# Attention's value products and exponential sums as one whole-array fp32 matmul for each head and key tile

## The chip, the cores and the metric

The kernel runs on 1 core of one Trainium2 chip. The metric is device time in microseconds (us) for one execution. The core has five engines that run their own instruction lists in order and wait for each other by semaphores: PE (TensorE, matmuls into PSUM), DVE (VectorE), ACT (ScalarE), POOL (GpSimd) and SP, whose queue issues the DMAs. The profile shows PE's weight loads as an engine of their own, PEld.

## The reference

Two layers work on 1024 latent and 256 context tokens of 1024 channels. Each layer has a modulated RMS norm, one input projection, three token mixers side by side (Fourier mixing, attention, a gated linear recurrence called HGRN), an output projection and a SwiGLU feed-forward part. The change touches the attention alone: 8 query heads, 2 key/value heads, 64 channels each. Latent queries read all 1280 keys; in layer 0 the 256 context queries read the 256 context keys.

```python
def attend(q, k, v):
    s = jnp.einsum('bkgqd,bksd->bkgqs', q, k).astype(jnp.float32) * (HEAD_DIM ** -0.5)
    p = jax.nn.softmax(s, axis=-1).astype(v.dtype)
    return jnp.einsum('bkgqs,bksd->bkgqd', p, v)
```

So for each head and query the kernel needs the exponentials p of its scores, their sum over the keys, the sum over the keys of p times V, and the quotient of the last two.

## The kernel before

The kernel is written in a framework that records the operations in program order and lets a scheduler set the order of each engine's list; tiles live in pools, and a tile waits for a buffer of its pool. `five` is a pool of 25 SBUF buffers of 128 x 1280 fp32. In PSUM it uses eight tiles (banks, in what follows) of 128 x 512 fp32, in four tags of two: `mm`, `sc`, `mx`, `pv`.

Layer by layer, `mixers` projects the inputs, `values` makes V (10 key tiles of 128 keys, both kv heads side by side: 128 keys x 128 columns), `keys` makes K1 and K2, and `queries` the queries. Then come the attention units. A unit is one pair of query heads j (0 to 3; kv head g = j // 2) and one chunk of queries ci: 0 is the 256 context queries, 1 and 2 are 512 latent queries each. Layer 0 has 12 units, layer 1 has 8. `unit_attend` runs over the unit's key tiles kt (10, or 2 for ci = 0): for each of the two heads a, two fp32r matmuls (L631, L632) make the scores `sc` with keys on the partitions, and ACT makes p = exp(scores) (L634). One key tile later follow the value products, L640: for head a the stationary operand is 64 columns of V, the moving operand p (fp32), and the result goes to the half `64*a` of one bank `pv`, so that the two heads stand in the two column halves of the array. After every second key tile come four sums, L645: the stationary operand `first` is 32 columns, a one and 31 zeros, so each adds up p of one head and one key tile in a quarter of the array's columns, into rows 0, 32, 64 and 96 of a second bank `sm`.

At a unit's end ACT copies both banks to SBUF (`pvs`, `sms`), and `unit_finish`, called one key tile into the next unit, lets one matmul with the block matrix `blk` add the quarter sums and spread them over 64 rows (L661). ACT then takes the logarithm and exp(-x) (L663, L664), DVE multiplies (L665), and SP writes the result to `dmix`.

Between the key tiles the loop in `mixers` steps two generators: `unit_prepare` for the unit two ahead, whose matmuls `mx` (L597) and DVE maxima (L598) find a bound for the scores, and `other`, the HGRN and Fourier work, at RATE 1.1 or 1.07 steps for each key tile. HGRN has products `lp` that use quarters of the array (64 x 64), products `ho` with 64 columns (L870) and whole-array products (L851, L855, L867). An fp32 matmul is recorded as two matmuls (two passes), an fp32r matmul as one. L131 to L133 are the three products of the helper `mm3`, which all projections use.

Of the kernel before, what the change touches and what calls it, by code (L numbers as in the profile page):

```python
# [10 lines left out]
F32 = mybir.dt.float32  # L11
F32R = mybir.dt.float32r
U8 = mybir.dt.uint8
AF = mybir.ActivationFunctionType
# [4 lines left out]
P = 128  # L19
# [64 lines left out]
ACB = 5  # L84
# [15 lines left out]
class Kern:  # L100
# [44 lines left out]
    def consts(self):  # L145
        nc, C, I = self.nc, self.C, self.I
        self.c = {}
        cv = self.t2("cv")[0:16, 0:P]
        nc.sync.dma_start(out=cv[0:8], in_=I["c"].rearrange("o (k p) -> (o k) p", p=P))
        nc.sync.dma_start(out=cv[8:16], in_=I["c_ctx"].rearrange("(k p) -> k p", p=P))  # L150
        self.c["ident"] = self.cst.tile([P, P], F32, name="c_ident")
        nc.sync.dma_start(out=self.c["ident"], in_=C["ident"])
        self.last_silu = nc.scalar.activation(out=cv, in_=cv, func=AF.Silu).ins
        ptr = self.ps("mx", "ptc")
        nc.tensor.transpose(ptr[:, 0:16], cv, self.c["ident"][0:16, 0:16])
        sc32 = self.cst.tile([P, KD, 32], F32, name="sc32")
        nc.vector.memset(sc32, 0.0)
        nc.vector.tensor_copy(out=sc32[:, :, 0:2], in_=ptr[:, 0:16].rearrange("p (v k) -> p k v", v=2))
        self.sc32 = sc32
        ones = self.cst.tile([P, P], F32, name="ones")  # L160
        nc.vector.memset(ones, 1.0)
        self.c["ones"] = ones
        first = self.cst.tile([P, 32], F32, name="first")
        nc.vector.memset(first, 0.0)
        nc.vector.memset(first[:, 0:1], 1.0)
        self.c["first"] = first
        eps = self.cst.tile([P, 1], F32, name="eps")
        nc.vector.memset(eps, EPS)
        self.eps = eps
# [369 lines left out]
    def values(self, l):  # L539

        nc = self.nc
        W = 384
        wh, wl = self.wv
        self.V = self.five(f"V{l}", shape=(P, 10, P))
        for t in range(10):
            acc = self.ps("mm", f"v{l}_{t}")
            ts = slice(t * P, (t + 1) * P)
            self.mm3(acc[:, :W], [(self.hh[k][:, ts], self.hl[k][:, ts], wh[k], wl[k]) for k in range(KD)])
            nc.scalar.copy(out=self.V[:, t], in_=acc[:, 0:P])
            vi = self.t2("vi")  # L550
            nc.vector.tensor_copy(out=vi[:, 0:256], in_=acc[:, P:W])
            nc.sync.dma_start(out=self.dv[t], in_=vi[:, 0:256])
# [62 lines left out]
    def unit_attend(self, l, j, ci, Q1, Q2):  # L615


        nc = self.nc
        g = j // 2
        n = CHUNKS[ci][1]  # L620
        nk = 2 if ci == 0 else 10
        pv = self.ps("pv", f"pv{j}_{ci}")
        sm = self.ps("pv", f"sm{j}_{ci}")
        ps = []
        for kt in range(nk + 1):
            if kt < nk:
                ks = slice(kt * P, (kt + 1) * P)
                p = []
                for a in range(2):
                    sc = self.ps("sc", "sc")  # L630
                    nc.tensor.matmul(sc[:, :n], self.K1[g][:, ks], Q1[a], start=True, stop=False)  # L631
                    nc.tensor.matmul(sc[:, :n], self.K2[g][0:66, ks], Q2[a][0:66], start=False, stop=True)  # L632
                    pf = self.t2(f"p{a}", tag="pa", bufs=PAB)[:, :n]
                    nc.scalar.activation(out=pf, in_=sc[:, :n], func=AF.Exp, scale=0.125)  # L634
                    p.append(pf)
                ps.append(p)
            if kt:
                i = kt - 1
                for a in range(2):
                    nc.tensor.matmul(pv[64 * a:64 * a + 64, :n], self.V[:, i, 64 * g:64 * g + 64], ps[i][a], start=(i == 0), stop=(i == nk - 1))  # L640
                if i % 2:
                    for a in range(2):
                        for o in range(2):
                            r = 64 * a + 32 * o
                            nc.tensor.matmul(sm[r:r + 32, :n], self.c["first"], ps[i - 1 + o][a], start=(i == 1), stop=(i == nk - 1), tile_position=(0, r))  # L645
            if kt == DELAY and self.pending:
                self.pending()
                self.pending = None
            yield
        if self.pending:  # L650
            self.pending()
        pvs, sms = [self.t2(nm, tag="acc", bufs=ACB)[:, :n] for nm in ("pvs", "sms")]
        nc.scalar.copy(out=pvs, in_=pv[:, :n])
        nc.scalar.copy(out=sms, in_=sm[:, :n])
        self.pending = lambda: self.unit_finish(j, ci, pvs, sms)

    def unit_finish(self, j, ci, pvs, sms):
        nc = self.nc
        n = CHUNKS[ci][1]
        sm = self.ps("mx", "sm")  # L660
        nc.tensor.matmul(sm[:, :n], self.c["blk"], sms)  # L661
        r = self.t2("ar")[:, :n]
        nc.scalar.activation(out=r, in_=sm[:, :n], func=AF.Ln)  # L663
        nc.scalar.activation(out=r, in_=r, func=AF.Exp, scale=-1.0)  # L664
        nc.vector.tensor_tensor(out=r, in0=pvs, in1=r, op=ALU.mult)  # L665
        nc.sync.dma_start(out=self.dmix[2 + j, :, CHUNKS[ci][0]:CHUNKS[ci][0] + n], in_=r)
# [864 lines left out]
```

## Time and profile before

| | |
|---|---|
| median of 3 runs | 3270.12 us (3266.48 to 3270.54) |
| the profiled execution | 3264.48 us, span 3262.7 us |
| PE busy | 3143.9 us (96%) |
| DVE busy | 1983.9 us (61%) |
| ACT busy | 1403.6 us (43%) |
| POOL busy | 109.0 us (3%) |
| attention of layer 0 | 347 to 780 us of the span |
| attention of layer 1 | 2085 to 2452 us of the span |

A busy PE says only that some matmul was in flight: matmuls are pipelined and their ends are modelled, so they overlap in the records. What a matmul costs PE is better read from starts: from its own start to the start of the next one.

### The profile page before, as it was taken

How to read it: one execution, taken by the hardware profiler on the slowest of the kernel's cores; microseconds unless marked ns; L12 is line 12 of the kernel's file. 1: busy time of each engine (PE TensorE's matmuls, PEld its weight loads, DVE VectorE, ACT ScalarE, POOL GpSimd, SP SyncE). 2: the span in 40 equal slices, each digit the busy share in tenths (PEclk: the TensorE clock that was granted, in tenths of full speed). 3: DMA queues.
4: the chain of work that ended last, by engine and by line, in shares of the span. 5: the costliest groups of instructions: out<-in, count | busy, mean ns of one | idle time of the engine just before them, and what ended most of it. 6: DMA issues, size and time to landing. Idle time of an engine off the chain costs nothing.

```text
span 3262.7 us, 44741 instructions
## 1 busy us (share of the span) xinstructions
PE 3143.9 (96%) x16826; PEld 2322.2 (71%) x16826; DVE 1983.9 (61%) x3459; ACT 1403.6 (43%) x2538; POOL 109.0 (3%) x85
## 2 busy tenths in 40 slices
PE   7999999998979999998999999999999799999998
PEld 4977544455858888886887997544557588887887
DVE  5298766653487666665437427677533876667343
ACT  5255455454353232333335435455453533334343
POOL 1000000000120000000001000000001200000000
PEclk9999999999989999998999999999999899999999
DMA  8356101024314333337645433111025122225453
GB/s 278 110 157 212 49 23 71 20 84 162 118 43 126 97 106 117 108 122 248 189 141 163 147 114 99 54 64 32 30 81 187 49 94 88 80 84 167 147 174 94
DMA packets 358657, 369.51 MB, mean 113 GB/s; under 512 B 21896, under 2 KB 268072, under 8 KB 358440
## 3 DMA queue, kind: packets, MB, share of 16 engines
q1 hardware_dynamic: 358440, 366.65, 35.3%
q8 instruction: 132, 2.16, 0.3%
q14 instruction: 85, 0.70, 0.1%
HBM read 282.00 MB, written 84.41 MB: 112 GB/s over the span
## 4 chain that ended last, share of the span: by engine, by line
PE 84%; DVE 7%; DMA 4%; ACT 3%; issue 1%; SPq 0%; POOL 0%; DVEq 0%; ACTq 0%; POOLq 0%
PE fp L131 8%; PE fp L133 8%; PE fp L132 8%; PE pv L640 6%; PE fd L131 5%; PE fd L133 5%; PE fd L132 5%; PE mx L597 3%; PE sm L645 3%; PE sc L631 3%; PE u L131 3%; PE u L132 3%; PE u L133 3%; PE sc L632 2%; PE oacc L132 2%; PE oacc L131 2%
## 5 line engine op out<-in xcount | busy, mean ns | idle before, releaser
L131 PE MATMUL fd<-a,hwd 128*128 128x512 f32 (+1 forms) x880 | 327.3, 372 | 14.7 <-ACT hwd L124 14.7
L133 PE MATMUL fd<-a,lwd 128*128 128x512 f32 (+1 forms) x880 | 327.6, 372 | 7.2 <-DVE lwd L125 7.0
L132 PE MATMUL fd<-a,hwd 128*128 128x512 f32 (+1 forms) x880 | 325.5, 370 | 0.0
L125 DVE TENSOR_TENSOR lwd<-rwd,hwd 128x512 fp32r<-128x512 f32 (+1 forms) x240 | 158.5, 662 | 267.0 <-ACT hwd L124 258.6
L598 DVE TENSOR_REDUCE mp<-mx 128x1 f32<-128x512 f32 (+1 forms) x400 | 224.1, 591 | 134.0 <-PE mx L597 132.6
L124 ACT CAST hwd<-rwd 128x512 fp32r<-128x512 f32 (+1 forms) x240 | 140.2, 584 | 308.1 <-PE fd L132 173.4
L634 ACT ACTIVATE p<-sc 128x512 f32<-128x512 f32 (+1 forms) x336 | 186.1, 586 | 193.4 <-PE sc L632 185.3
L640 PE MATMUL pv<-p,V 128*64 128x512 f32 (+1 forms) x672 | 232.7, 606 | 0.0
L131 PEld LDWEIGHTS fd<-a,hwd 128*128 128x128 f32 x880 | 167.9, 191 | 43.0 <-ACT hwd L124 15.3
L133 PEld LDWEIGHTS fd<-a,lwd 128*128 128x128 f32 x880 | 167.6, 190 | 37.3 <-DVE lwd L125 9.7
L132 PEld LDWEIGHTS fd<-a,hwd 128*128 128x128 f32 x880 | 167.9, 191 | 27.7 <-issue 0.2
L278 DVE SCALAR_TENSOR_TENSOR as<-wa,sc,as 128x512 f32<-128x512 f32 x224 | 161.3, 748 | 35.5 <-DMA wa<-in_w_ada_dram 34.6
L131 PE MATMUL fp<-mh,hw_gate 128*128 128x512 f32 x352 | 141.1, 401 | 7.0 <-ACT hw_gate L124 7.0
L133 PE MATMUL fp<-mh,lw_gate 128*128 128x512 f32 x352 | 140.1, 398 | 6.3 <-DVE lw_gate L125 6.3
L132 PE MATMUL fp<-ml,hw_gate 128*128 128x512 f32 x352 | 139.3, 396 | 0.0
L131 PE MATMUL fp<-mh,hw_up 128*128 128x512 f32 x352 | 137.8, 392 | 0.0
L132 PE MATMUL fp<-ml,hw_up 128*128 128x512 f32 x352 | 137.7, 391 | 0.0
L133 PE MATMUL fp<-mh,lw_up 128*128 128x512 f32 x352 | 137.0, 389 | 0.0
L131 PE MATMUL u<-a0hh,hwin 128*128 128x512 f32 (+1 forms) x360 | 132.8, 371 | 3.8 <-ACT a0hh L331 2.1
L132 PE MATMUL u<-a0hl,hwin 128*128 128x512 f32 (+1 forms) x360 | 129.4, 361 | 4.1 <-POOL a0hl L329 2.5
L131 PE MATMUL oacc<-mh,hwo 128*128 128x512 f32 (+1 forms) x320 | 121.3, 380 | 9.5 <-ACT mh L124 9.5
L133 PE MATMUL u<-a0hh,lwin 128*128 128x512 f32 (+1 forms) x360 | 127.9, 357 | 0.0
(359 smaller groups left out, 7423.2 us busy)
## 6 DMA issues: line engine op xcount, KB each, us to landing
rwd<-in_w_down_dram SPq DMA_DIRECT2D x200, 256.0 KB
wa<-in_w_ada_dram SPq DMA_DIRECT2D x192, 256.0 KB
rw_gate<-in_w_gate_dram SPq DMA_DIRECT2D x44, 512.0 KB
rw_up<-in_w_up_dram SPq DMA_DIRECT2D x44, 512.0 KB
da<-mw_gate SPq DMA_DIRECT2D x88, 256.0 KB
ar<-da SPq DMA_DIRECT2D x88, 256.0 KB
rwin<-in_w_in_dram SPq DMA_DIRECT2D x30, 512.0 KB
rwo<-in_w_out_dram SPq DMA_DIRECT2D x24, 512.0 KB
```

The lines of the kernel that those rows point to most:

```text
L124: self.nc.scalar.copy(out=hi, in_=src)
L125: self.nc.vector.tensor_tensor(out=lo, in0=src, in1=hi, op=ALU.subtract)
L131: self.nc.tensor.matmul(out, lh, rh, start=(first and i == 0), stop=False)
L132: self.nc.tensor.matmul(out, lh, rl, start=False, stop=False)
L133: self.nc.tensor.matmul(out, ll, rh, start=False, stop=(last and i == n - 1))
L278: nc.vector.scalar_tensor_tensor(out=acc, in0=w, scalar=sc, in1=acc, op0=ALU.mult, op1=ALU.add)
L597: nc.tensor.matmul(mx[:, :kn], Q1[a][:, t * P:(t + 1) * P], self.K1[g][:, k0:k0 + kn])
L598: nc.vector.tensor_reduce(out=mp[:, a * nt + t, i:i + 1], in_=mx[:, :kn], axis=AX.X, op=ALU.max)
L631: nc.tensor.matmul(sc[:, :n], self.K1[g][:, ks], Q1[a], start=True, stop=False)
L634: nc.scalar.activation(out=pf, in_=sc[:, :n], func=AF.Exp, scale=0.125)
L640: nc.tensor.matmul(pv[64 * a:64 * a + 64, :n], self.V[:, i, 64 * g:64 * g + 64], ps[i][a], start=(i == 0), stop=(i == nk - 1))
L645: nc.tensor.matmul(sm[r:r + 32, :n], self.c["first"], ps[i - 1 + o][a], start=(i == 1), stop=(i == nk - 1), tile_position=(0, r))
```

## The change

V is kept in two tiles, one for each kv head: columns 0 to 63 are V, columns 64 to 127 are ones, set by POOL. One fp32 matmul for each head and key tile uses all 128 columns: rows 0 to 63 of the result are the value product, rows 64 to 127 all hold the sum of p. So the sums of every second key tile, `first`, and the matmul with `blk` go. The two banks of tag `pv` now belong to the two heads. At a unit's end ACT reads each bank twice: a copy of the value half and a logarithm of the sum half, each on 64 partitions. Layer 0's and layer 1's `values` copy V in two pieces of 64 columns.

```diff
@@ consts
-        first = self.cst.tile([P, 32], F32, name="first")
-        nc.vector.memset(first, 0.0)
-        nc.vector.memset(first[:, 0:1], 1.0)
-        self.c["first"] = first
@@ values
-        self.V = self.five(f"V{l}", shape=(P, 10, P))
+        self.V = [self.five(f"V{l}_{g}", shape=(P, 10, P)) for g in range(2)]
+        for V in self.V:
+            nc.gpsimd.memset(V[:, :, 64:P], 1.0)
...
-            nc.scalar.copy(out=self.V[:, t], in_=acc[:, 0:P])
+            for g in range(2):
+                nc.scalar.copy(out=self.V[g][:, t, 0:64], in_=acc[:, 64 * g:64 * g + 64])
@@ unit_attend
-        pv = self.ps("pv", f"pv{j}_{ci}")
-        sm = self.ps("pv", f"sm{j}_{ci}")
+        pv = [self.ps("pv", f"pv{j}_{ci}_{a}") for a in range(2)]
...
                 for a in range(2):
-                    nc.tensor.matmul(pv[64 * a:64 * a + 64, :n], self.V[:, i, 64 * g:64 * g + 64], ps[i][a], start=(i == 0), stop=(i == nk - 1))
-                if i % 2:
-                    for a in range(2):
-                        for o in range(2):
-                            r = 64 * a + 32 * o
-                            nc.tensor.matmul(sm[r:r + 32, :n], self.c["first"], ps[i - 1 + o][a], start=(i == 1), stop=(i == nk - 1), tile_position=(0, r))
+                    nc.tensor.matmul(pv[a][:, :n], self.V[g][:, i], ps[i][a], start=(i == 0), stop=(i == nk - 1))
...
-        pvs, sms = [self.t2(nm, tag="acc", bufs=ACB)[:, :n] for nm in ("pvs", "sms")]
-        nc.scalar.copy(out=pvs, in_=pv[:, :n])
-        nc.scalar.copy(out=sms, in_=sm[:, :n])
-        self.pending = lambda: self.unit_finish(j, ci, pvs, sms)
+        pvs, r = [self.t2(nm, tag="acc", bufs=ACB)[:, :n] for nm in ("pvs", "lns")]
+        for a in range(2):
+            nc.scalar.copy(out=pvs[64 * a:64 * a + 64], in_=pv[a][0:64, :n])
+            nc.scalar.activation(out=r[64 * a:64 * a + 64], in_=pv[a][64:P, :n], func=AF.Ln)
+        self.pending = lambda: self.unit_finish(j, ci, pvs, r)
@@ unit_finish
-        sm = self.ps("mx", "sm")
-        nc.tensor.matmul(sm[:, :n], self.c["blk"], sms)
-        r = self.t2("ar")[:, :n]
-        nc.scalar.activation(out=r, in_=sm[:, :n], func=AF.Ln)
```

The scheduler orders the new program afresh. Outside the two attention stages, the values stage and a few POOL, ACT and DMA rows around them, the lists are the same.

First, PE in the third unit of layer 0 (j = 0, ci = 2). Before, around the value products of its third key tile (`sc` are scores, `mx` the bounds for a later unit, `lp` HGRN products, `pv` value products, `sm` sums):

```order
L632 MATMUL sc<-Qwl_3336,K_0_0_1484 128x512
L597 MATMUL mx<-K_0_0_1482,Q_3766 128x512
L640 MATMUL pv_2_3939<-p_4019,V_1187 64x512
L597 MATMUL mx<-K_0_0_1482,Q_3766 128x512
L597 MATMUL mx<-K_0_0_1482,Q_3766 128x256
L640 MATMUL pv_2_3939<-p_4024,V_1187 64x512
L631 MATMUL sc<-Qwh_3333,K_0_0_1482 128x512
L632 MATMUL sc<-Qwl_3335,K_0_0_1484 128x512
```

And now, around those of its fourth:

```order
L597 MATMUL mx<-K_0_0_1492,Qwh_3943 128x256
L639 MATMUL pv_2_0_3925<-p_4034,V_0_1184 128x512
L597 MATMUL mx<-K_0_0_1492,Qwh_3942 128x256
L639 MATMUL pv_2_1_3926<-p_4039,V_0_1184 128x512
L597 MATMUL mx<-K_0_0_1492,Qwh_3943 128x256
L789 MATMUL lp<-W_00_3373,kk_0_3377 64x64 x8
L630 MATMUL sc<-Qwh_3343,K_0_0_1492 128x512
L631 MATMUL sc<-Qwl_3345,K_0_0_1494 128x512
```

In both, other matmuls stand between the two heads' value products. Before, each such product (64 rows of output, 64 columns of the array) stands alone between whole-array matmuls; now it has 128 rows like its neighbours.

Second, ACT at the end of the first unit of layer 0. Before (`kk` are HGRN copies, `Qwl` and `Q` operands of coming units):

```order
L613 CAST Qwl_3335<-rows 2x512
L653 COPY pvs<-pv_1_3316 128x512
L654 COPY sms<-sm_1_3317 128x512
L613 CAST Qwl_3336<-rows 2x512
L634 ACTIVATE p_3754<-sc 128x256
L634 ACTIVATE p_3759<-sc 128x256
```

And now:

```order
L613 CAST Qwl_3345<-rows 2x512
L648 COPY pvs<-pv_1_0_3326 64x512
L613 CAST Qwl_3346<-rows 2x512
L649 ACTIVATE lns<-pv_1_0_3326 64x512
L648 COPY pvs<-pv_1_1_3327 64x512
L649 ACTIVATE lns<-pv_1_1_3327 64x512
L633 ACTIVATE p_3746<-sc 128x256
L633 ACTIVATE p_3751<-sc 128x256
```

Four reads of PSUM instead of two stand ahead of the next unit's first exponentials.

Third, POOL in layer 0 while the normalised inputs of the latent chunk ci = 1 are split (`a0hl` is the low part of one 128-channel block). Before:

```order
L329 TENSOR_TENSOR a0hl_171<-hf,a0hh_163 128x512
L329 TENSOR_TENSOR a0hl_173<-hf,a0hh_165 128x512
L329 TENSOR_TENSOR a0hl_175<-hf,a0hh_167 128x512
L329 TENSOR_TENSOR a0hl_169<-hf,a0hh_161 128x512
L329 TENSOR_TENSOR a0hl_171<-hf,a0hh_163 128x512
```

And now:

```order
L325 TENSOR_TENSOR a0hl_168<-hf,a0hh_160 128x512
L325 TENSOR_TENSOR a0hl_170<-hf,a0hh_162 128x512
L543 MEMSET V_0_1184 128x10x64
L543 MEMSET V_1_1185 128x10x64
L325 TENSOR_TENSOR a0hl_172<-hf,a0hh_164 128x512
L325 TENSOR_TENSOR a0hl_166<-hf,a0hh_158 128x512
```

The two memsets stand ahead of the chunk's last block; each waits for a buffer whose last reader is DVE's first or second operation on the next chunk.

## Rows read from the trace of the kernel before

**Rows 1.** The page's part 1: busy time, share of the span, instructions.

```profile
PE 3143.9 (96%) x16826; PEld 2322.2 (71%) x16826; DVE 1983.9 (61%) x3459; ACT 1403.6 (43%) x2538; POOL 109.0 (3%) x85
```

**Rows 2.** The page's part 4: the chain that ended last, by engine.

```profile
PE 84%; DVE 7%; DMA 4%; ACT 3%; issue 1%; SPq 0%; POOL 0%; DVEq 0%; ACTq 0%; POOLq 0%
```

**Rows 3.** Busy time by stretch: the attention stages, and a stretch of layer 1.

```profile
core 0: us, PE busy (x) PEld busy (x) DVE busy (x) ACT busy (x) POOL busy (x), PEclk, DMA share, GB/s
347.00:780.00 433.00, 428.49 (x3020) 211.63 (x3019) 259.92 (x567) 222.60 (x411) 2.27 (x2) 1.00 0.15 46
...
2085.00:2452.00 367.00, 362.95 (x2503) 176.67 (x2500) 221.57 (x451) 186.07 (x323) 2.27 (x2) 1.00 0.15 46
2250.00:2300.00 50.00, 49.70 (x497) 23.71 (x496) 40.31 (x84) 24.04 (x42) 0.00 (x0) 1.00 0.10 25
```

**Rows 4.** Groups of PE instructions by form, 347 to 2452 us: count, busy us, mean ns.

```profile
L640 PE MATMUL pv<-p,V 128*64 128x512 f32 x640 | 225.6, 617 | 0.0
...
L645 PE MATMUL sm<-p,first 128*32 128x512 f32 x640 | 106.0, 605 | 0.0
...
L661 PE MATMUL sm<-sms,c_blk 128*128 128x512 f32 x32 | 17.7, 635 | 1.4 <-ACT sms L654 1.4
```

**Rows 5.** Timeline of PE near 416 us: start, duration in us, instruction, count.

```profile
415.99 0.40 PE L632 MATMUL sc<-Qwl,K 66*128 66x512 f32 x1
416.22 0.40 PE L597 MATMUL mx<-K,Q 128*128 128x512 f32 x1
416.55 1.07 PE L640 MATMUL pv<-p,V 128*64 128x512 f32 x2
...
418.10 1.07 PE L640 MATMUL pv<-p,V 128*64 128x512 f32 x2
419.10 0.50 PE L631 MATMUL sc<-Qwh,K 128*128 128x512 f32 x1
419.44 0.40 PE L632 MATMUL sc<-Qwl,K 66*128 66x512 f32 x1
419.68 0.40 PE L631 MATMUL sc<-Qwh,K 128*128 128x512 f32 x1
```

**Rows 6.** Timeline of PE near 2346 us.

```profile
2345.54 1.02 PE L876 MATMUL oss<-osq,c_blk 128*128 128x512 f32 x2
2346.49 1.08 PE L640 MATMUL pv<-p,V 128*64 128x512 f32 x4
2347.50 1.06 PE L645 MATMUL sm<-p,first 128*32 128x512 f32 x8
2348.50 0.73 PE L597 MATMUL mx<-K,Q 128*128 128x512 f32 x2
```

**Rows 7.** Timeline of PE near 394 us, a unit of 256 queries.

```profile
393.98 0.65 PE L640 MATMUL pv<-p,V 128*64 128x256 f32 x2
394.56 0.39 PE L631 MATMUL sc<-Q,K 128*128 128x256 f32 x1
```

**Rows 8.** Timeline of ACT at the first unit's end.

```profile
391.02 0.58 ACT L653 COPY pvs<-pv 128x512 f32<-128x512 f32 x1
391.50 0.59 ACT L654 COPY sms<-sm 128x512 f32<-128x512 f32 x1
...
397.40 0.60 ACT L663 ACTIVATE ar<-sm 128x512 f32<-128x512 f32 x1 [1.66 <-PE sm L661]
```

**Rows 9.** Groups of ACT, 347 to 2452 us: count, busy, mean ns, idle before and its cause.

```profile
L634 ACT ACTIVATE p<-sc 128x512 f32<-128x512 f32 (+1 forms) x334 | 185.0, 586 | 187.0 <-PE sc L632 185.3
```

**Rows 10.** Timeline of POOL while the inputs of layer 0 are split.

```profile
67.08 3.49 POOL L329 TENSOR_TENSOR a0hl<-hf,a0hh 128x512 fp32r<-128x512 f32 x2 [3.21 <-ACT a0hh L328]
73.12 3.47 POOL L329 TENSOR_TENSOR a0hl<-hf,a0hh 128x512 fp32r<-128x512 f32 x2 [2.55 <-ACT a0hh L328]
...
86.00 2.27 POOL L506 MEMSET K<- 64x1280 f32 x2
```

**Rows 11.** The tile of V's projections: ACT's copy, count and duration in ns.

```profile
L549 ACT COPY V<-v x20: 265/266/266, 124.0 to 1946.7; 128x128 f32<-128x128 f32 x20
```

More of the change, by code (lines that the diff above doesn't have):

```diff
@@ L651, in unit_attend, with unit_finish @@
             self.pending()
-        pvs, sms = [self.t2(nm, tag="acc", bufs=ACB)[:, :n] for nm in ("pvs", "sms")]
-        nc.scalar.copy(out=pvs, in_=pv[:, :n])
-        nc.scalar.copy(out=sms, in_=sm[:, :n])
-        self.pending = lambda: self.unit_finish(j, ci, pvs, sms)
-    def unit_finish(self, j, ci, pvs, sms):
+        pvs, r = [self.t2(nm, tag="acc", bufs=ACB)[:, :n] for nm in ("pvs", "lns")]
[3 more added lines that the diff above has]
+        self.pending = lambda: self.unit_finish(j, ci, pvs, r)
+    def unit_finish(self, j, ci, pvs, r):
         nc = self.nc
         n = CHUNKS[ci][1]
-        sm = self.ps("mx", "sm")
-        nc.tensor.matmul(sm[:, :n], self.c["blk"], sms)
-        r = self.t2("ar")[:, :n]
-        nc.scalar.activation(out=r, in_=sm[:, :n], func=AF.Ln)
         nc.scalar.activation(out=r, in_=r, func=AF.Exp, scale=-1.0)
```

## The prediction

> **What bounds the kernel now.** I read the busy times first: PE is busy 96% of the span, DVE 61%, ACT 43% [rows 1]. The chain that ended last lies to 84% on PE [rows 2]. The table by stretch then places the change: the two attention stages last 433 and 367 us, together 800 us, with PE busy about 99% at the full granted clock (1.00), DVE 260 and 222 us, ACT 223 and 186 us [rows 3]. So in these stages a microsecond taken from PE is a microsecond of the kernel, until DVE or ACT is late. ACT's exponentials wait 185 us for the scores that PE makes [rows 9]; the reader is to see that ACT follows PE there, not the reverse. Outside the stages PE does what it did before.
>
> **Streaming.** The groups by form show how much PE work is in question: 640 recorded passes of value products and 640 of sums with 512 queries, mean 617 and 605 ns [rows 4]. These means contain overlap, so I take starts. A whole-array fp32 matmul with 512 columns (the norm sum `oss`) starts at 2345.54, what follows at 2346.49: 0.95 us, of which 0.09 belong to what follows (below), so 0.86 us. Four recorded passes of `pv`, both heads beside each other, take 1.01 (2346.49 to 2347.50), eight of `sm`, four matmuls beside each other, 1.00 [rows 6]. But two passes of `pv`, one head alone, also take 1.00 (418.10 to 419.10) [rows 5]. Half an array costs what a whole one costs, unless the other half is filled. How often it is, PE's order tells. Before, with 512 queries, the value products stand in 101 runs of one, 96 of two, 1 of three and 6 of four: 101 + 96 + 2 + 12 = 211 times one after another. The sums stand in 19 runs of one, 79 of two to four and 2 of five: 102 times. With `blk`'s 16 that makes 329. With 256 queries there are 11 + 6 + 4 = 21, at 0.58 - 0.14 = 0.44 us [rows 7]. After: 320 and 16 whole-array matmuls. Saved: 9 x 0.86 + 5 x 0.44 = 10 us. By streaming alone the change is nearly even.
>
> The Trainium skill speaks against the change here: "TensorEngine Tiling (Array Packing)", section Performance Considerations, advises 2x column tiling where the stationary operand has at most 64 columns, and its overview puts the gain at up to 2x. By that rule the 336 value products would have cost 160 x 0.86 + 8 x 0.44 = 141 us before, not 186, and streaming would grow by 35 us instead of falling by 10. The trace agrees only where two heads stand side by side, 1.01 us for both; the lone run of one head cost 1.00.
>
> **Changing the array's form.** Here the trace shows the larger term. In one form, scores follow each other at 0.24 us (419.44 to 419.68). The last matmul ahead of a `pv` takes 0.33 (416.22 to 416.55), where `mx` or `sc` otherwise takes 0.23 (415.99 to 416.22): 0.09 to leave a form. The first matmul after `pv` takes 0.34 (419.10 to 419.44) instead of 0.24: 0.10 to enter the whole array. `pv` alone takes 1.00 - 0.86 - 0.09 = 0.05 more to enter 64 columns [rows 5]; `sm` 1.00 - 0.86 - 0.09 = 0.05, of which part is its eight starts, so 0.04 to enter 32 columns [rows 6]. A change thus costs 0.19 into the whole array, 0.14 into 64 columns, 0.13 into 32, and I take 0.14 for HGRN's quarters, which no row here isolates (0.09 if entering is free, 0.19 if it costs as much as the whole array). Counted in PE's order within the two stages:
>
> into whole array: 326 before, 141 after: 185 x 0.19 = 35 us
> into 64 columns: 224 and 10: 214 x 0.14 = 30 us
> into 32 columns: 106 and 0: 106 x 0.13 = 14 us
> into quarters: 139 and 131: 8 x 0.14 = 1 us
>
> Together 795 changes become 282, worth 80 us. What is left are HGRN's own products. PE's work falls by 80 + 10 = 90 us of 800.
>
> **What is given back.** ACT at a unit's end: before, two copies of 0.58 and 0.59 and later a logarithm of 0.60 [rows 8]; after, four reads on 64 partitions. The trace shows no such 64-partition read of 512 columns from PSUM, so between half (0.3) and the same (0.6); the maxima and exponentials of 512 columns lie near 0.59 [rows 9], so I take 0.6. That is 0.6 us more ACT work at each of 20 ends, 12 us, and the exponentials of the next unit come up to 1.2 us later, as the four reads stand ahead of them. Bounds: 0 (other matmuls stand between) to 20 x 1.2 = 24 us. I take half a microsecond for each: 10 us. No cost for the longer hold of the `pv` banks beside this: the next unit's first value product needs those same exponentials.
>
> DVE: its work stays, PE's shrinks by 90/800 = 11%. Over the stages its share rises from 60% to 68%; in the densest stretch, 2250 to 2300, 40.3 of 50 us become 40.3 of about 44.4 [rows 3], 91%. The maxima that free the `mx` banks will then stand behind HGRN's multiplications now and then. Bounds: 0 to 35 us, the latter if PE got only half of its gain in both stages after the ACT term. I take 4 us, since only this stretch comes near.
>
> POOL: two memsets stand ahead of the last block of chunk 1, whose operation began at 73.12. A memset of 1280 columns takes 1.13 us (2.27 for two) [rows 10]; the new ones have 640 columns on all partitions, 0.6 to 1.1 each. POOL waited 2.55 us there, but the second memset needs DVE's work on the next chunk. Bounds 0 to 2.3; I take 1 us, as the products behind this block wait in turn. In layer 1 the memsets stand ahead of the last context blocks, which come only after the down projection's end: nothing. V's copies become two of at most 0.27 us for each tile [rows 11], while PE spends 24 products on the tile: ACT hides them. The second V takes one more of the 25 buffers; HGRN's two forget-gate loads of a layer then both start at the last projection's end instead of one, ahead of work that begins several key tiles later. Nothing, or up to 4 us for each layer if that load is late.
>
> **Sum.** -80 - 10 + 10 + 4 + 1 = -75. Against the profiled execution: 3264.5 - 75 = 3189.5 us. The median of the runs lies 5.6 us above that execution, so the forecast is 3195 us, 2.3% faster. A difference under 0.2% (6.5 us) can't be told from none.
>
> **Rivals.**
> 1. DVE and ACT become the next bound in both stages and take back half of the gain: 3270 - 90 + 24 + 20 + 1 = 3225. For it: 91% in one stretch. Against: 68% over the stages, and value products free p earlier, since no sum holds the even key tile's p any longer.
> 2. The 0.19 us are not the price of a change but of late weights that will be late anyway: only the 10 of streaming and the 15 given back are left, 3275, no change. Against: the price appears at every `pv` row shown, and scores among scores don't have it.
> 3. The lone heads did share the array with their neighbours, and their starts hide it: streaming grows by 35 instead of falling by 10, 3195 + 45 = 3240. For it: the other half of the array is free. Against: the next start comes as late as after a pair. This is where the Trainium skill's rule in "TensorEngine Tiling (Array Packing)" would lead.
> 4. Slower: each value product waits for its exponential. Place: ACT, every key tile. Two exponentials take 1.2 us; if two more ACT operations (1.2 us) come between scores and products at each of 168 key tiles, 202 us are lost and the time is 3270 - 90 + 202 = 3382; it turns to slower from 90/168 = 0.54 us for each key tile. For it: the products follow only one key tile behind. Against: ACT is half idle and waits for PE.
>
> **Chances.** Forecast 0.77, its own range 3175 to 3212: from nothing given back and 5 us more for the changes of form (3180 - 5) to 32 us given back. Rival 1 0.12, rival 2 0.03, rival 3 0.03, rival 4 0.05. The range for 8 in 10 reaches into rival 1: 3172 to 3230. Faster 0.92, the same 0.03, slower 0.05.
>
> **What would show it.** PE's group `pv` has 640 passes whose next start comes 0.43 later, `sm` and `blk` are gone; scores before and after `pv` show 0.24, not 0.33; the stages last about 392 and 333 us; all else keeps its length. Wrong: PE idle before value products or `mx` in sum over 30 us, DVE's share near 90% throughout, or the 0.33 still beside a whole-array `pv`.

## The result: 92.5 us faster, and the profile after

The changed kernel took 3177.85 us (median of 4 runs, 3174.92 to 3185.0) against 3270.33 us before on the same chip; the ratio is 0.972, 95% interval 0.9708 to 0.9731. The forecast was 3195 us: direction and range hold, and the gain is 17 us larger than forecast. The profiled execution took 3176.2 us.

Busy times and the chain by engine, from the page of the changed kernel, against [rows 1, 2]:

```profile
PE 3048.2 (96%) x16114; PEld 2378.9 (75%) x16114; DVE 1976.1 (62%) x3457; ACT 1414.2 (45%) x2578; POOL 114.0 (4%) x89
...
PE 81%; DVE 8%; ACT 4%; DMA 4%; issue 2%; SPq 1%; POOL 0%; DVEq 0%; ACTq 0%; POOLq 0%
```

PE lost 96 us of work and is still the bound. The attention stages from their first value product to their last, by stretch (length, then busy time of PE, PEld, DVE, ACT and POOL, then the granted clock). Before:

```profile
347.00:774.00 427.00, 425.22 (x3007) 210.43 (x3005) 258.28 (x562) 218.99 (x403) 2.27 (x2) 1.00 0.15 47
2075.00:2447.00 372.00, 370.54 (x2542) 180.06 (x2545) 226.31 (x459) 188.23 (x327) 2.27 (x2) 1.00 0.15 47
```

And after:

```profile
347.00:733.00 386.00, 376.75 (x2642) 239.92 (x2640) 269.04 (x586) 235.26 (x438) 2.27 (x2) 1.00 0.21 69
2018.00:2369.00 351.00, 341.93 (x2224) 213.78 (x2223) 234.25 (x476) 200.93 (x350) 2.27 (x2) 1.00 0.22 71
```

PE's idle time, length less busy time, was 1.8 and 1.5 us and is 9.3 and 9.1: 15 us more. DVE's share rises to 70 and 67%.

The groups of value products and unit ends after, for [rows 4, 8] (count, busy, mean ns, idle before):

```profile
L639 PE MATMUL pv<-p,V 128*128 128x512 f32 x640 | 307.6, 593 | 0.0
```

```profile
L648 ACT COPY pvs<-pv x40: 362/578/582, 386.1 to 2369.2; 64x512 f32<-64x512 f32 x32, 64x256 f32<-64x256 f32 x8
L649 ACT ACTIVATE lns<-pv x40: 378/592/596, 387.3 to 2369.8; 64x512 f32<-64x512 f32 x32, 64x256 f32<-64x256 f32 x8
```

The two groups of sums are gone. A read of 64 partitions of PSUM costs ACT what one of 128 costs (0.58 and 0.59 us).

Where the 88.5 us of the two spans went, by the starts of PE's instructions: up to the first value product of layer 0, 347.9 and now 347.8 us. From there to its last value product, 425.7 and 385.0: 40.7 saved. From there to the first gate product of the feed-forward part, a stretch that is mainly the output projection, 129.2 and 113.2: 16.0 saved. From layer 1's first value product to its first gate product, 470.7 and 438.2: 32.5 saved. All the rest is equal within 1.2 us. The 16.0 us were not in the forecast.

### The profile page after: what moved, and what is told of

The parts are those of the page before. It is cut to its first block, busy times and chain, and to the rows that moved or that the text cites. A ratio compares the mean times of both kernels' runs of the same rounds, so it can differ in the third digit from the quotient of the medians.

```text
span 3174.2 us, 43396 instructions
## 1 busy us (share of the span) xinstructions
PE 3048.2 (96%) x16114; PEld 2378.9 (75%) x16114; DVE 1976.1 (62%) x3457; ACT 1414.2 (45%) x2578; POOL 114.0 (4%) x89
## 4 chain that ended last, share of the span: by engine, by line
PE 81%; DVE 8%; ACT 4%; DMA 4%; issue 2%; SPq 1%; POOL 0%; DVEq 0%; ACTq 0%; POOLq 0%
PE fp L131 8%; PE fp L133 8%; PE fp L132 8%; PE pv L639 7%; PE fd L131 5%; PE fd L132 5%; PE fd L133 5%; PE u L131 3%; PE u L132 3%; PE u L133 3%; PE mx L597 2%; PE sc L630 2%; PE sc L631 2%; PE oacc L132 2%; PE oacc L131 2%; PE oacc L133 2%
## 5 line engine op out<-in xcount | busy, mean ns | idle before, releaser
L639 PE MATMUL pv<-p,V 128*128 128x512 f32 (+1 forms) x672 | 316.0, 584 | 0.0
L132 PEld LDWEIGHTS fd<-a,hwd 128*128 128x128 f32 x880 | 168.9, 192 | 27.7 <-issue 0.2
L639 PEld LDWEIGHTS pv<-p,V 128*128 128x128 f32 x672 | 122.7, 189 | 77.9 <-issue 62.7
```

The source lines that it names most:

```text
L132: self.nc.tensor.matmul(out, lh, rl, start=False, stop=False)
L639: nc.tensor.matmul(pv[a][:, :n], self.V[g][:, i], ps[i][a], start=(i == 0), stop=(i == nk - 1))
```

## The experiments

Each ratio stands against the kernel before in the same session (3269 to 3271 us). Distances from the changed kernel are taken to its 3177.85 us, and single distances of under 4 us are within the intervals.

**quotient_in_t2.** The quotient's tile goes back to the buffers in which the output projection loads its operand.

```
-pvs, r = [self.t2(nm, tag="acc", bufs=ACB)[:, :n] for nm in ("pvs", "lns")]
+pvs = self.t2("pvs", tag="acc", bufs=ACB)[:, :n]
+r = self.t2("ar")[:, :n]
```

> The changed kernel with one tile moved back: the buffer r of the reciprocal sums comes from tag t2 again, as in the kernel before, instead of tag acc. In the list of SP this puts 20 of the 24 loads of the output projection's inputs of layer 0 behind the last unit's write again. Theory (the out projection began earlier because r left t2: layer 0 by 11 us, layer 1 by 5): the time returns by about 16 us, to 3194, with the first output products of each layer waiting for ACT's casts as in the kernel before. Rival (the out projection began earlier because the attention stage became shorter): no change, 3178.

Measured: 3219.47 us, ratio 0.9845 (0.983 to 0.986), 41.6 us slower than the changed kernel and 25 more than the theory's 3194. The time from layer 0's last value product to its first gate product is back at 131.8 us. SP's queue shows why. First the changed kernel, its loads of the operand (`mixf`) and its stores of quotients (`dmix<-lns`):

```profile
673.86 4.18 SPq L996 DMA_DIRECT2D mixf<-dmix  x5
...
696.22 2.22 SPq L657 DMA_DIRECT2D dmix<-lns  x2
...
701.57 6.24 SPq L996 DMA_DIRECT2D mixf<-dmix  x4
...
710.61 8.89 SPq L996 DMA_DIRECT2D mixf<-dmix  x7
...
720.06 4.25 SPq L996 DMA_DIRECT2D mixf<-dmix  x5
...
727.72 0.97 SPq L996 DMA_DIRECT2D mixf<-dmix  x2
...
736.45 0.32 SPq L657 DMA_DIRECT2D dmix<-lns  x1
...
741.35 0.32 SPq L996 DMA_DIRECT2D mixf<-dmix  x1
```

The kernel before, same queue:

```profile
757.55 2.93 SPq L1005 DMA_DIRECT2D mixf<-dmix  x4
...
779.07 0.32 SPq L666 DMA_DIRECT2D dmix<-ar  x1
779.49 3.96 SPq L1005 DMA_DIRECT2D mixf<-dmix  x7
...
784.05 5.07 SPq L1005 DMA_DIRECT2D mixf<-dmix  x5
...
791.33 3.11 SPq L1005 DMA_DIRECT2D mixf<-dmix  x5
...
797.60 2.81 SPq L1005 DMA_DIRECT2D mixf<-dmix  x3
```

There are five buffers. Before, four loads and the last unit's quotient (`ar`) take them, and the other 20 loads stand behind its store, which comes 5.5 us after the last value product (773.6). After, 23 of 24 loads are issued ahead of that store. In quotient_in_t2 the order is four, the store, 7, 5, 5 and 3 again. That returns 18.6 us here, and layer 1, up to its first gate product, 15.8 (454.0 instead of 438.2); another 9.4 us lie within layer 0's attention (394.4 instead of 385.0), and no run isolates their cause. The edit does more than put the tile back: here the logarithm that first writes `ar` runs at the unit's end, and from its start to the store a median of 7.3 us passes, where it was 2.3 in the kernel before. PE's waits for exponentials in the two stages are 14.2 us here and 6.9 in the changed kernel. So 42 us is not the price of the tag alone.

**before_quotient_in_acc.** The kernel before, with the quotient written over the summed exponentials' tile, which is not one of these buffers.

```
-r = self.t2("ar")[:, :n]
+r = sms
```

> The kernel before with one tile moved: the logarithm of the sums is written over the copy sms, in tag acc, instead of a new tile of t2. Nothing else of the change is in it. Theory (the tag): 3270 - 16 = 3254. Rival (the shorter attention stage): 3270, no change.

Measured: 3251.86 us, ratio 0.9947 (0.9933 to 0.9962): 19.3 us faster by this line alone. From layer 0's last value product to its first gate product it takes 116.2 us instead of 129.2, and from layer 1's first value product to its first gate product 465.9 instead of 470.7. PE at the start of the output projection (start, duration, idle ahead and its releaser), before:

```profile
775.90 1.12 PE L661 MATMUL sm<-sms,c_blk 128*128 128x512 f32 x2 [0.70 <-ACT sms L654]
778.67 0.39 PE L131 MATMUL oacc<-mh,hwo 128*128 128x256 f32 x1 [1.64 <-ACT mh L124]
779.44 0.58 PE L132 MATMUL oacc<-ml,hwo 128*128 128x256 f32 x1 [0.38 <-DVE ml L125]
779.82 0.41 PE L133 MATMUL oacc<-mh,lwo 128*128 128x256 f32 x1
780.03 0.41 PE L131 MATMUL oacc<-mh,hwo 128*128 128x256 f32 x1
```

The changed kernel:

```profile
729.87 3.60 PE L639 MATMUL pv<-p,V 128*128 128x512 f32 x8
732.91 0.68 PE L131 MATMUL oacc<-mh,hwo 128*128 128x256 f32 x1
733.43 0.28 PE L132 MATMUL oacc<-ml,hwo 128*128 128x256 f32 x1
733.54 0.28 PE L133 MATMUL oacc<-mh,lwo 128*128 128x256 f32 x1
```

The wait costs twice: PE stands idle, and behind it the same products start 0.21 us apart instead of 0.12. From 780 to 785 us the granted clock was 0.50, the lower of its two levels (1.2 instead of 2.4 GHz); over the whole stretch it was 0.97 before:

```profile
773.00:903.00 130.00, 121.37 (x597) 99.03 (x595) 59.02 (x92) 53.20 (x95) 18.24 (x15) 0.97 0.49 159
```

and 1.00 after, where PE went from attention to the projection without a pause:

```profile
733.00:846.00 113.00, 112.62 (x582) 95.79 (x581) 46.08 (x70) 41.61 (x72) 18.50 (x15) 1.00 0.38 122
```

So 13 of the unforecast 16 us have their cause: the change took the quotient out of the buffers that the next stage needs.

**form_64_columns.** The changed kernel with value products of 64 columns, both heads in the same half of the array.

```
-matmul(pv[a][:, :n], self.V[g][:, i], ps[i][a], ...)
+matmul(pv[a][0:64, :n], self.V[g][:, i, 0:64], ps[i][a], ...)
...
-nc.scalar.activation(out=r[64 * a:64 * a + 64], in_=pv[a][64:P, :n], func=AF.Ln)
+nc.scalar.activation(out=r[64 * a:64 * a + 64], in_=pv[a][0:64, :n], func=AF.Exp, scale=0.01)
```

> The changed kernel with value products of 64 columns, both heads in columns 0 to 63, so that nothing runs side by side and PE's order is that of the changed kernel; the sums are left out (ACT takes an exponential of the value half where the logarithm of the sums was, with the same shape). The passes stream the same columns, only the form of the array changes 656 times instead of 282. Theory (each change costs 0.19 into the whole array, 0.14 into 64 columns): 168 x 0.19 + 206 x 0.14 = 61 us more, 3239. Rival (the 0.09 and 0.10 beside a value product are late weights, which are late in any form): 3178.

Measured: 3226.99 us, ratio 0.9869 (0.9854 to 0.9883), 49 us slower than the changed kernel, of the 61 that the price gives. PE, the changed kernel:

```profile
415.72 0.40 PE L631 MATMUL sc<-Qwl,K 66*128 66x512 f32 x1
415.96 1.88 PE L639 MATMUL pv<-p,V 128*128 128x512 f32 x4
417.27 0.79 PE L630 MATMUL sc<-Qwh,K 128*128 128x512 f32 x1
417.90 0.40 PE L631 MATMUL sc<-Qwl,K 66*128 66x512 f32 x1
```

form_64_columns:

```profile
422.44 0.40 PE L631 MATMUL sc<-Qwl,K 66*128 66x512 f32 x1
422.77 1.93 PE L639 MATMUL pv<-p,V 128*64 128x512 f32 x4
424.63 0.51 PE L630 MATMUL sc<-Qwh,K 128*128 128x512 f32 x1
424.97 0.40 PE L631 MATMUL sc<-Qwl,K 66*128 66x512 f32 x1
```

Without a change of form a matmul's start is shown while the last pass still runs, so one compares the second start behind the products: 417.90 - 415.72 = 2.18 us against 424.97 - 422.44 = 2.53. A visit is one stay of PE among the value products. Over layer 0, medians of 62, 106 and 12 visits: 0.235 and 0.330 us from the last score to the first pass, 0.432 and 0.480 for that pass, 0.661 and 0.863 for the last pass with the first of two scores behind it. That is 0.095 + 0.048 + 0.202 = 0.345 us for a visit, where the forecast had 0.19 + 0.14 = 0.33; the passes between take 0.429 us in both. PE's idle time in the stages falls by 9 us here (9.2 and 9.1 to 5.3 and 4.0), so most of the 12 us that are missing from 61 had been waits.

**form_64_halves.** As form_64_columns, but head 0 in the lower and head 1 in the upper half of the array.

```
-matmul(pv[a][:, :n], self.V[g][:, i], ps[i][a], ...)
+matmul(pv[a][64 * a:64 * a + 64, :n], self.V[g][:, i, 0:64], ps[i][a], ...)
...
```

> As form_64_columns, but the second head's product stands in columns 64 to 127, so that neighbouring products of the two heads can run side by side; the sums are left out too. The scheduler's order now has 175 lone products and 66 runs of two to four (249 one after another with 512 queries instead of 320) and 735 changes of form. Theory (only neighbours in the list share the array): 3178 + 73 us of form - 71 x 0.86 - 3 x 0.44 = 3189. Rival (a lone head shares the array with its neighbours as well, so that all 168 pairs cost one product): 175 lone products cost half, 75 us less, 3114.

Measured: 3199.5 us, ratio 0.978 (0.9763 to 0.9798), 22 us slower than the changed kernel, 10 slower than the theory and 85 slower than the rival. Not all of the 22 is the form: the granted clock was 0.97 and 0.99 in the two stages, where the changed kernel had 1.00, and by these shares some 15 us is an estimate of what the lower level took. A lone head's two passes still take 1.00 us to the next start (421.15 to 422.15):

```profile
420.83 0.39 PE L631 MATMUL sc<-Qwl,K 66*128 66x512 f32 x1
421.15 1.07 PE L639 MATMUL pv<-p,V 128*64 128x512 f32 x2
422.15 0.27 PE L605 MATMUL mt<-c_ident,m 128*8 128x128 f32 x1
```

The Trainium skill's advice of column tiling for at most 64 columns ("TensorEngine Tiling (Array Packing)", section Performance Considerations) is borne out only where the other half's product stands next in PE's order. The Trainium skill's section Tiling Modes on the same page says that changing the mode drains the engine. The rows of form_64_columns are in keeping with it, though ends are modelled: the first score behind the products starts at 424.63, about as the last pass ends (422.77 + 1.93 = 424.70), where without a change it starts well before (417.27, with the end at 415.96 + 1.88 = 417.84).

**unit_end_copies_on_vector.** The 40 copies at the unit ends go to DVE.

```
-nc.scalar.copy(out=pvs[64 * a:64 * a + 64], in_=pv[a][0:64, :n])
+nc.vector.tensor_copy(out=pvs[64 * a:64 * a + 64], in_=pv[a][0:64, :n])
```

> The changed kernel with the two copies of the value sums at each unit end on VectorE instead of ScalarE; the two logarithms stay. Theory of the prediction: the two additional ScalarE reads at each of 20 unit ends hold up the next unit's exponentials, 0.5 us each, 10 us in all; without them 3168 us. Rival: TensorE finds other work at the unit ends and the ScalarE term is about nothing; the 40 copies of 0.58 us on VectorE hide too, 3178 us within 4. Should VectorE be the engine that comes last at a unit end, 3178 + up to 23 = 3201.

Measured: 3175.4 us, ratio 0.9713 (0.97 to 0.9726). That can't be told from the changed kernel: moving the copies to DVE does not bring the 10 us. PE's waits for exponentials in the stages fall from 6.9 to 3.6 us, and those for DVE's maxima rise from 2.9 to 4.8.

**unit_end_reads_doubled.** The same copies, twice on ACT.

```
 nc.scalar.copy(out=pvs[64 * a:64 * a + 64], in_=pv[a][0:64, :n])
+nc.scalar.copy(out=pvs[64 * a:64 * a + 64], in_=pv[a][0:64, :n])
```

> The changed kernel with each of the 40 copies of the value sums at the unit ends issued twice on ScalarE, to the same place: 1.16 us more at each of 20 ends, 23 us of ScalarE. Theory of the prediction: about half of it shows, +10 us, 3188. Rival, the ScalarE term is about nothing: 3178 within 4.

Measured: 3194.15 us, ratio 0.9771 (0.9757 to 0.9784), 16 us slower: 0.8 us at each end for 1.16 us more. Neither line fits: moving the copies away gives nothing, adding reads costs more than half. PE's waits for exponentials go from 6.9 to 15.1 us. It looks as if the changed kernel had no slack left at the unit ends; no run measures how much there was before.

**half_the_maxima_twice.** The second head's maxima are taken twice.

```
 nc.vector.tensor_reduce(out=mp[:, a * nt + t, i:i + 1], in_=mx[:, :kn], ...)
+if a:
+    nc.vector.tensor_reduce(out=mp[:, a * nt + t, i:i + 1], in_=mx[:, :kn], ...)
```

> The changed kernel with the maximum of the second head of every key range taken twice on VectorE, to the same place: about 170 more reductions of 0.55 us within the two attention stages, 94 us of VectorE, whose share there rises from some 66% to some 79%. Theory: PE stays the bound, VectorE's waits grow by a few us, 3178 + 0 to 15. Rival (VectorE and ScalarE had become the next bound and kept part of the gain): most of the 94 us shows, 3178 + 50 to 94.

Measured: 3186.76 us, ratio 0.9749 (0.9736 to 0.9762). DVE has 85 us more in the stages (311.35 and 276.72 us for 269.04 and 234.25), 79% of them, and the kernel takes 9 us more:

```profile
349.00:745.00 396.00, 384.59 (x2643) 246.08 (x2642) 311.35 (x674) 235.65 (x438) 2.28 (x2) 0.98 0.22 71
2027.00:2379.00 352.00, 339.11 (x2210) 213.16 (x2208) 276.72 (x561) 203.41 (x351) 2.27 (x2) 0.99 0.21 70
```

PE's idle time rises by 6 us in the two stages. PE's busy time in layer 0 rises as well, by 7.8 us, with a granted clock of 0.98 there instead of 1.00. DVE was not the next bound.

**quarters_unsplit.** HGRN's quarter products, the form that is left, in longer runs.

```
-RATE = (1.1, 1.07)
+RATE = (0.91, 0.84)
...
-                if x == 3:
-                    yield
```

> The changed kernel without the yield that cuts HGRN's groups of 32 quarter products in two, and with the rate of these steps lowered in proportion (0.91 and 0.84 a key tile instead of 1.1 and 1.07), so that they spread over the attention stages as before. Same work; in PE's order the changes of the array's form within the stages fall from 282 to 216 (into quarters 131 to 98, into the whole array 141 to 108, into 64 columns 10 both). Theory (a change costs 0.19 into the whole array and 0.14 into quarters): 33 x 0.19 + 33 x 0.14 = 11 us less, 3167 us. Rival (a change into quarters and back costs nothing that PE's other waits don't cover, or the longer runs make HGRN's steps come late): 3178 or more.

Measured: 3176.83 us, ratio 0.9712 (0.9699 to 0.9726), 1 us less than the changed kernel and 10 above the theory. The stages:

```profile
348.00:734.00 386.00, 372.55 (x2640) 240.97 (x2638) 267.31 (x584) 236.00 (x438) 2.28 (x2) 0.99 0.22 72
2018.00:2368.00 350.00, 337.71 (x2226) 213.94 (x2226) 234.69 (x477) 202.62 (x351) 2.27 (x2) 0.99 0.22 70
```

PE's busy time fell by 4.2 us in each, 8.4 of the 11; its idle time rose from 9.3 and 9.1 to 13.5 and 12.3. The gain was there and became waits. Those for exponentials went only from 6.9 to 8.2 us, those for ACT's copies of the Fourier products (`za`, `yh`) from 3.3 to 9.0.

**quarters_unsplit_vector_copies.** Both edits together.

> quarters_unsplit and unit_end_copies_on_vector in one: HGRN's quarter products in runs twice as long at the lowered rate (0.91 and 0.84), and the copies of the value sums at the unit ends on VectorE. In quarters_unsplit the form changes went down by 66 and PE's waits, most of them for ScalarE's exponentials, rose by 7.5 us. Theory (these waits come from ScalarE, whose load the copies are part of): with 23 us of copies off ScalarE part of the 11 us comes through, 3178 - 2 - 5 = 3171 us. Rival (the waits come from the longer runs themselves: two score banks can't be filled while 32 quarter products run): 3175 to 3177, as each of the two alone.

Measured: 3170.1 us, ratio 0.9688 (0.9675 to 0.9701), where 3171 was expected. PE's idle time in the stages falls back from 25.7 to 18.1 us. The expectation put these waits mainly on the exponentials; the trace shows otherwise: those stay (8.9 us after 8.2), and the waits for `za` and `yh` are gone. Alone the two edits gave 1 and 2 us, within the intervals; together they give 8, which is clear of the changed kernel. That 8 is more than the sum of the two is not clear of the intervals, some 4 us each.

**quarters_unsplit_rate_kept.** The same with `RATE = (1.1, 1.07)` as in the changed kernel.

> As quarters_unsplit_vector_copies, but with the rate of HGRN's steps left at 1.1 and 1.07 a key tile, so that with fewer steps they come earlier and leave the last units of each attention stage alone. 202 form changes in PE's order (282 in the changed kernel, 214 in quarters_unsplit_vector_copies). Theory (the form price decides): 1 to 2 us less than quarters_unsplit_vector_copies, 3170 us. Rival (where HGRN's work is denser, PE waits more for ScalarE and VectorE, and the last units have less to fill the waits): 3180 or more.

Measured: 3163.95 us, ratio 0.9674 (0.966 to 0.9687), 14 us below the changed kernel, 6 below the theory's 3170, and the fastest here:

```profile
347.00:730.00 383.00, 375.36 (x2655) 240.28 (x2654) 278.18 (x607) 226.42 (x415) 2.27 (x2) 1.00 0.21 68
2015.00:2359.00 344.00, 336.56 (x2227) 212.02 (x2226) 243.32 (x492) 195.44 (x336) 2.33 (x2) 1.00 0.22 72
```

PE idles 7.6 and 7.4 us. The output projection's first product now starts 32 us ahead of layer 0's last value product (697.4, 729.4) and 53 us ahead in layer 1, where the changed kernel has 0 and 27. That this overlap is the cause of the last 6 us is likely, but no run isolates it.

## Why the prediction was right, step by step

**PE bounds both stages: right.** Work taken from PE shortened them, and 85 us more on DVE cost 9.

**Changes of form, 80 us: right in kind, and the main term.** form_64_columns puts 374 changes back and measures 49 us of 61, with the price of a visit as forecast. Rival 2, no price at all, would have left that kernel at 3178. No run isolates the changes into 32 columns, 14 us. The 0.14 for quarters is borne out only by PE's busy time: 8.4 us less for 11 forecast (quarters_unsplit).

**Streaming, 10 us: right in kind.** A whole-array pass takes 0.429 us, as a lone 64-column pass does. That the halves don't share time, rival 3's point, form_64_halves shows. No run isolates the 10 us.

**Given back, 10 + 4 + 1 = 15 us: right in sum, partly by luck.** PE's idle time in the stages rose by 15 us. The mechanism named for ACT is there, though smaller. PE's waits for the exponential that frees a score bank (who waited for whom: us in total, times, longest), before in layer 1 (in layer 0 none is listed), then after in layers 0 and 1:

```profile
PE sc L631 <- ACT p L634: 0.4, 2, 0.2
```

```profile
PE sc L630 <- ACT p L633: 3.0, 4, 1.3
...
PE sc L630 <- ACT p L633: 3.9, 6, 1.5
```

Of these 6.9 us, 6.0 come within 8 us after a read at a unit's end. One of them, ACT first, then PE:

```profile
694.06 0.38 ACT L649 ACTIVATE lns<-pv 64x256 f32<-64x256 f32 x1
694.46 1.09 ACT L633 ACTIVATE p<-sc 128x512 f32<-128x512 f32 x2
```

```profile
695.12 0.50 PE L630 MATMUL sc<-Q,K 128*128 128x512 f32 x1 [1.26 <-ACT p L633]
```

So ACT's term is some 6.5 us, not 10. (The prediction cites [rows 9] for the maxima too, but that row has the exponentials only; the reads did take the 0.6 us assumed.) The waits for DVE's maxima rose from 0.2 to 2.9 us, for 4 forecast. Another 2.8 us are more waits for ACT's copies `za`, which the forecast did not have. POOL's 1 us did not reach the attention: the next block now starts as the second memset ends, 6.68 us behind its predecessor where it was 6.04 (72.81 - 66.13, before 73.12 - 67.08 [rows 10]), but the first value product comes at 347.8 instead of 347.9:

```profile
70.89 0.63 POOL L543 MEMSET V<- 128x640 f32 x1 [1.27 <-DVE hf L321]
72.21 0.64 POOL L543 MEMSET V<- 128x640 f32 x1 [0.69 <-DVE hf L321]
72.81 3.50 POOL L325 TENSOR_TENSOR a0hl<-hf,a0hh 128x512 fp32r<-128x512 f32 x2
```

V's split copies cost nothing either: from layer 1's first V product to its first value product it took 170.3 us before and 169.6 after.

**The stages.** Layer 0's was to shorten by 41 us and did by 40.7. Layer 1's was to shorten by 34; up to the gate product it shortened by 32.5, but the output projection now begins inside it, so the two can't be parted cleanly. Against before_quotient_in_acc, which has the tile's new place already, layer 0's attention shortened by 42.9 us (427.9 to 385.0) and layer 1 up to the gate product by 27.7 (465.9 to 438.2): layer 1 gave some 6 us less than forecast.

**What failed: "all else keeps its length".** The diff moved the quotient from `t2` to `acc`, and the prediction priced the ACT operations on it but not the tile's place. before_quotient_in_acc gets 19 us from that place alone, 13.0 in layer 0's output projection and 4.8 ahead of layer 1's gate product, and the forecast was off by 17. What was priced comes out: from before_quotient_in_acc to the changed kernel it is 3251.86 - 3177.85 = 74 us, for 75 forecast. That it agrees so closely is in part luck, since form_64_columns fell short of its price, layer 1 gave less and layer 0 more. With the tile left in `t2` in the changed kernel (quotient_in_t2, held longer there), only 3271.2 - 3219.47 = 52 us are left, and that time lies outside the forecast's range: without the place, and with the hold, the forecast would have failed.

**Rivals 1 and 4.** DVE and ACT took back some 15 us, not half. 85 us more on DVE cost 9 (half_the_maxima_twice), but 23 us more on ACT at the unit ends cost 16 (unit_end_reads_doubled), so ACT is close to the bound there. Value products do not wait for exponentials: their group has 0.0 us of idle time ahead of it.

## What to carry to other kernels

Where a bound TensorE alternates between whole-array matmuls and narrow ones, count the changes of form in its order and price each from neighbouring starts; filling unused columns with something useful (here the sums) can be free. When a change moves a tile to another pool tag, ask who else waits for the old tag, above all the stage that starts next. A gain on PE can turn into a wait for an engine with half its time free: list PE's waits again after each step, since the next edit belongs to the one that has grown.

## What the runs showed of the hardware that was not expected

A visit to another form cost 0.345 us in form_64_columns, and the one lone pair of passes between scores cost as much as the runs of four. After PE's wait at the start of the output projection, products with 256 columns started 0.21 us apart at a granted clock of 0.50, instead of 0.12. ACT read 64 partitions of PSUM in the time of 128 (0.58 and 0.59 us), which the prediction had left open between half and the same.
